# A log-softmax on one core: the first three tiles are stored at once, the later ones half a tile late

## The chip, the core and the metric

The kernel runs on one core of a Trainium2 chip. The metric is device time in microseconds (us) of one launch. Ten runs of the kernel before the change gave 7587.55 to 7592.54 us, with a median of 7589.58 us.

## What is computed

The reference takes `x` of shape 16 x 512 x 50000 in float32 and computes a log-softmax over the last axis:

```
max_x = np.max(x, axis=-1, keepdims=True)
shifted = x - max_x
log_sum_exp = np.log(np.sum(np.exp(shifted), axis=-1, keepdims=True))
return shifted - log_sum_exp
```

Input and output have 1638.4 MB each. Every byte is read once and written once, so some 3277 MB pass between HBM and SBUF.

## The kernel before

**Tiling.** The 8192 rows of 50000 numbers are cut into 256 tiles of 32 rows. A row lies on four neighbouring partitions (G = 4), so a tile is 128 partitions x 12500 numbers, 6250 KB (6.4 MB). There are four buffers of that size in SBUF (NBUF = 4); tile t lives in buffer t mod 4, is loaded into it, changed in place and stored from it. Inside a tile the work on the numbers goes in four column pieces of 3125 (NS = 4).

**One tile, engine by engine.**

- SyncE (SP) issues the load (L147). The first four loads need no wait. Each later load into a buffer waits until the store from that buffer has landed (`take(sync, stored[j])`, L47).
- VectorE (DVE) waits for the landing (L47) and takes the negated maximum of each of the four pieces (L197). Some small instructions then agree on one maximum per row (L202, L165, L168, L174, L180).
- ScalarE (ACT) computes the exponentials of a piece, with their sum, as soon as the maximum of that piece is there (L239, four per tile). It then computes four correction factors (L247).
- DVE multiplies sums by factors (L208), TensorE adds them up across a row's partitions (L277), ACT takes the logarithm (L227), and DVE subtracts maximum and logarithm from the whole tile in place (L185).
- The store is a DMA that ACT issues (L231). It waits on the semaphore `subtracted` until DVE has subtracted that tile.

**Order.** Each engine has its own program and runs it in order; the semaphores tie them together. There is no scheduler: the order on each engine is the one written. On DVE the tiles follow one another without interleaving: maxima of tile t, subtraction of tile t, maxima of tile t+1. On ACT the store of a tile stands inside the work of the next tile, between its second and its third exponential (GATE = 2):

```
for c in range(NS):
    if c == GATE and dst is not None:
        store((j - 1) % NBUF, dst, bufs[(j - 1) % NBUF])
    shifted.next(scalar.activation(out=dump, ...))
```

So the store of tile t is issued only after half of the exponentials of tile t+1. The last tile is different: it is subtracted and stored in four pieces, and the store of the tile before it is put ahead of its exponentials.

**Loops.** DVE and TensorE run a loop of 63 rounds of four tiles and then four more tiles written out. SP writes out the first four loads and loops 63 times over four loads. ACT writes out tile 0, loops 63 times over four tiles (1, 2, 3 and 0 of the next four), and writes out the last three. Because semaphores only count up, each engine ends a round with `settle`, which waits for what it has counted and takes that amount off again.

Loads go through the queue that the profile calls q1, stores through q10.

Of the kernel before, what the change touches and what calls it, by code (L numbers as in the profile page):

```python
# [19 lines left out]
NBUF = 4  # L20
# [29 lines left out]
def cols(c):  # L50
    return slice(c * C, (c + 1) * C)
# [3 lines left out]
def kernel(  # L55
# [11 lines left out]
    ntiles = N // R  # L67


    rounds = (ntiles - NBUF) // NBUF  # L70
# [3 lines left out]
    ot = of.rearrange("(t r) (g w) -> t (r g) w", r=R, g=G)  # L74

    def run(a, first, n):

        part = a[first : first + NBUF * n].rearrange("(q i) p w -> q i p w", i=NBUF)
        return lambda q, i: part[bass.ds(q, 1), i].rearrange("o p w -> (o p) w")
# [13 lines left out]
    bufs = [data.tile([P, W], FP32, name=f"buf{j}") for j in range(NBUF)]  # L93
# [37 lines left out]
    @block.gpsimd  # L131
    def _(gpsimd):
        view = ones.rearrange("p (r g) -> p r g", g=G)
        gpsimd.memset(ones, 1.0).then_inc(ready)  # L134
        gpsimd.affine_select(  # L135
            out=view, in_=view, pattern=[[-G, R], [0, G]], base=0,
            channel_multiplier=1, compare_op=ALU.is_ge, fill=0.0,
        ).wait_op(ready, 1, "sem-ge").then_inc(ready)
        gpsimd.affine_select(  # L139
            out=view, in_=view, pattern=[[G, R], [0, G]], base=G - 1,  # L140
            channel_multiplier=-1, compare_op=ALU.is_ge, fill=0.0,
        ).wait_op(ready, 2, "sem-ge").then_inc(ready)
# [80 lines left out]
    @block.scalar  # L223
    def _(scalar):
        def log(k):
            added.next(
                scalar.activation(out=logs[k], in_=rowsums[k], func=ACT.Ln)  # L227
            ).then_inc(logged.sem)

        def store(j, dst, buf):  # L230
            subtracted.next(scalar.dma_start(out=dst, in_=buf)).then_inc(stored[j], 16)  # L231

        def whole(j, dst=None):
# [4 lines that stand above are left out]
                shifted.next(  # L238
                    scalar.activation(  # L239
                        out=dump, in_=bufs[j][:, cols(c)], func=ACT.Exp,  # L240
                        bias=negms[j][:, c : c + 1], scale=1.0,
                        accum_out=parts[j][:, c : c + 1],
                    )
                ).then_inc(on_act.sem)
                on_act.next(scalar.nop())  # L245
            agreed.next(
                scalar.activation(  # L247
                    out=scales[j], in_=negms[j], func=ACT.Exp,
                    bias=negmaxs[j][:, 0:1], scale=-1.0,
                )  # L250
            ).then_inc(rescaled.sem)
            log(j)

        def settle():
            for count in (on_act, shifted, agreed, added, subtracted):
                count.settle(scalar)

        nc.scalar.preload_act_table_set("natural_log_exp_and_others")  # L258
        whole(0)
        settle()  # L260
        dst = run(ot, 0, rounds)
        with scalar.Fori(0, rounds) as q:
            for i in range(NBUF):
                whole((i + 1) % NBUF, dst(q, i))
            settle()
        for t in range(ntiles - NBUF + 1, ntiles - 1):
            whole(t % NBUF, ot[t - 1])
        store(t % NBUF, ot[t], bufs[t % NBUF])
        whole(NBUF - 1)
        for c in range(NS):  # L270
            store(NBUF - 1, ot[ntiles - 1][:, cols(c)], bufs[NBUF - 1][:, cols(c)])
# [50 lines left out]
```

## Time and profile before

| what | value |
|---|---|
| median of 10 runs | 7589.58 us (7587.55 to 7592.54) |
| the profiled execution | 7589.23 us, span 7587.5 us |
| DVE busy | 5440.4 us, 72% of the span |
| ACT busy | 3184.6 us, 42% |
| PE busy | 477.8 us, 6% |
| maxima, L197 | 1024 times, 3400 ns each |
| exponentials, L239 | 1024 times, 2868 ns each |
| subtraction of a whole tile, L185 | 6.79 us |
| bytes | 1638.40 MB read, 1638.40 MB written, 432 GB/s over the span |
| loads, issue to landing | median 36.7 us |
| stores of whole tiles, issue to landing | median 41.6 us |

The span is the time that the profile covers; 1.7 us of the profiled execution lie outside it. Busy time of an engine counts the instructions that compute; issuing a DMA and waiting are not in it. In the rows of windows further down, the columns are: the stretch in us from the span's start, its length, the busy time of PE, PE's weight loads, DVE, ACT and POOL with the number of instructions, TensorE's granted clock, the mean busy share of the 16 DMA engines, and GB/s. In the rows of a timeline they are: start, duration, engine, line, operation, output and inputs; in square brackets stands the idle time ahead of it and what ended it.

### The profile page before, as it was taken

How to read it: one execution, taken by the hardware profiler on the slowest of the kernel's cores; microseconds unless marked ns; L12 is line 12 of the kernel's file. 1: busy time of each engine (PE TensorE's matmuls, PEld its weight loads, DVE VectorE, ACT ScalarE, POOL GpSimd, SP SyncE). 2: the span in 40 equal slices, each digit the busy share in tenths (PEclk: the TensorE clock that was granted, in tenths of full speed). 3: DMA queues.
4: the chain of work that ended last, by engine and by line, in shares of the span. 5: the costliest groups of instructions: out<-in, count | busy, mean ns of one | idle time of the engine just before them, and what ended most of it. 6: DMA issues, size and time to landing. Idle time of an engine off the chain costs nothing. (4 is left out here: it accounts for less than half of the span.)

```text
span 7587.5 us, 13821 instructions
## 1 busy us (share of the span) xinstructions
PE 477.8 (6%) x2048; PEld 455.9 (6%) x2048; DVE 5440.4 (72%) x2819; ACT 3184.6 (42%) x2561; POOL 1.4 (0%) x7
## 2 busy tenths in 40 slices
PE   0000000000000000000000000000000000000000
PEld 0000000000000000000000000000000000000000
DVE  7777777777777777777777777777777777777776
ACT  4434444344443434444344443434444344444433
POOL 0000000000000000000000000000000000000000
DMA  9999999999999999999999999999999999999999
GB/s 417 433 433 431 433 434 432 433 434 433 433 434 434 431 434 434 432 433 434 434 432 434 434 432 434 434 432 434 434 434 432 434 433 432 434 434 431 434 434 399
DMA packets 74162, 3276.85 MB, mean 432 GB/s; under 512 B 8240, under 2 KB 8240, under 8 KB 8240
## 3 DMA queue, kind: packets, MB, share of 16 engines
q1 hardware_dynamic: 36864, 1638.42, 50.0%
q10 hardware_dynamic: 37296, 1638.42, 50.0%
q14 instruction: 2, 0.02, 0.0%
HBM read 1638.40 MB, written 1638.40 MB: 432 GB/s over the span
## 5 line engine op out<-in xcount | busy, mean ns | idle before, releaser
L239 ACT ACTIVATE dump<-buf,negm 128x3125 f32<-128x3125 f32 x1024 | 2937.3, 2868 | 3804.4 <-DVE negm L197 3765.0
L197 DVE TENSOR_REDUCE negm<-buf 128x1 f32<-128x3125 f32 x1024 | 3418.2, 3400 | 922.7 <-DVEq L47 922.7
L185 DVE TENSOR_SCALAR buf<-buf,negmax,logsum 128x12500 f32<-128x12500 f32 (+1 forms) x259 | 1738.8, 6714 | 553.6 <-ACT logsum L227 553.6
L277 PE MATMUL sums<-scaled,ones 128*128 128x1 f32 x2048 | 477.8, 355 | 7086.5 <-DVE scaled L208 7086.5
L277 PEld LDWEIGHTS sums<-scaled,ones 128*128 128x128 f32 x2048 | 455.9, 327 | 7108.3 <-DVE scaled L208 7108.3
L208 DVE TENSOR_TENSOR scaled<-scale,part 128x4 f32<-128x4 f32 x256 | 41.6, 162 | 580.4 <-ACT scale L247 580.4
L227 ACT ACTIVATE logsum<-sums 128x1 f32<-128x1 f32 x256 | 43.8, 171 | 550.9 <-PE sums L277 550.9
L239 ACT ACTIVATION_READ_ACCUMULATOR dump<-buf,negm 128x1 f32 x1024 | 190.8, 186 | 0.0
L247 ACT ACTIVATE scale<-negm,negmax 128x4 f32<-128x4 f32 x256 | 76.1, 297 | 23.6
L202 DVE TENSOR_REDUCE negp<-negm 128x1 f32<-128x4 f32 x256 | 40.1, 157 | 39.2 <-DVE negm L197 39.2
L180 DVE STREAM_TRANSPOSE negmax<-spread 128x32 f32<-128x32 f32 x256 | 54.2, 212 | 8.9
L165 DVE STREAM_TRANSPOSE allneg<-negp 128x32 f32<-128x32 f32 x256 | 54.1, 211 | 8.9
L168 DVE TENSOR_REDUCE rowneg<-allneg 128x8 f32<-128x32 f32 x256 | 47.6, 186 | 8.9
L174 DVE COPY spread<-rowneg 128x32 f32<-128x32 f32 x256 | 46.3, 181 | 8.9
L258 ACT ACT_TABLE_LOAD x1 | 1.3, 1283 | 1.0 <-SPq L111 1.0
L139 POOL TENSOR_SCALAR_AFFINE_SELECT ones<-ones 128x128 f32<-128x128 f32 x1 | 0.5, 520 | 0.1
L135 POOL TENSOR_SCALAR_AFFINE_SELECT ones<-ones 128x128 f32<-128x128 f32 x1 | 0.5, 519 | 0.1
L134 POOL MEMSET ones<- 128x128 f32 x1 | 0.2, 205 | 0.5 <-SPq L111 0.5
L306 POOL MEMSET const-uint8-127<- 128x1 uint8 x1 | 0.1, 103 | 0.0
L306 POOL MEMSET const-bfloat16-1.0<- 128x1 bf16 x1 | 0.1, 102 | 0.0
L306 POOL MEMSET const-float32-0.0<- 128x1 f32 x1 | 0.1, 100 | 0.3 <-issue 0.3
L306 POOL MEMSET const-float32-1.0<- 128x1 f32 x1 | 0.1, 100 | 0.0
## 6 DMA issues: line engine op xcount, KB each, us to landing
buf<-in_x_dram SPq DMA_DIRECT2D x256, 6250.0 KB, 36.7
out_dram<-buf ACTq DMA_DIRECT2D x255, 6250.0 KB, 41.6
out_dram<-buf ACTq DMA_DIRECT2D x4, 1562.5 KB, 11.3
```

What stands on the lines that cost most here:

```text
L165: vector.transpose(out=allneg, in_=negp.to_broadcast([P, SQ]))
L168: vector.tensor_reduce(out=rowneg, in_=allneg.rearrange("p (r g) -> p r g", g=G), op=ALU.min, axis=AX,)
L174: vector.tensor_copy(out=spread.rearrange("p (r g) -> p r g", g=G), in_=rowneg[:, :, None].to_broadcast([P, SQ // G, G]),)
L180: vector.transpose(out=negmaxs[k], in_=spread)
L185: ins = vector.tensor_scalar(out=buf, in0=buf, scalar1=negmaxs[k][:, 0:1], scalar2=logs[k], op0=ALU.add, op1=ALU.subtract,)
L197: vector.tensor_reduce(out=negms[j][:, c : c + 1], in_=bufs[j][:, cols(c)], op=ALU.max, axis=AX, negate=True,).then_inc(shifted.sem if c < ...
L202: vector.tensor_reduce(out=negp, in_=negms[j], op=ALU.min, axis=AX).then_inc(on_dve.sem)
L208: vector.tensor_mul(out=scaleds[j], in0=scales[j], in1=parts[j])
L227: scalar.activation(out=logs[k], in_=rowsums[k], func=ACT.Ln)
L239: scalar.activation(out=dump, in_=bufs[j][:, cols(c)], func=ACT.Exp, bias=negms[j][:, c : c + 1], scale=1.0, accum_out=parts[j][:, c : c + 1],
L247: scalar.activation(out=scales[j], in_=negms[j], func=ACT.Exp, bias=negmaxs[j][:, 0:1], scale=-1.0,)
L277: ins = tensor.matmul(rowsums[j], ones, scaleds[j][:, c : c + 1], start=c == 0, stop=c == NS - 1,)
```

## The change

Only ACT's program changes. Tiles 0, 1 and 2 are stored as soon as DVE has subtracted them: on ACT, the store of tile t now stands right behind the logarithm of tile t and ahead of the first exponential of tile t+1. From tile 3 on a store stands where it stood, between the second and the third exponential of the next tile.

For this, four tiles instead of one are written out ahead of ACT's loop, the loop has 62 rounds instead of 63 and goes over tiles 0, 1, 2 and 3 of a round, and four tiles instead of three are written out behind it. `settle` on ACT now follows the last tile of a group of four, where it followed the first one. There are 259 store DMAs as before, to the same places; the programs of SP, DVE, TensorE and GpSimd are the same.

```
         nc.scalar.preload_act_table_set("natural_log_exp_and_others")
-        whole(0)
+
+        for t in range(NBUF - 1):
+            whole(t)
+            store(t, ot[t], bufs[t])
+        whole(NBUF - 1)
         settle()
-        dst = run(ot, 0, rounds)
-        with scalar.Fori(0, rounds) as q:
-            for i in range(NBUF):
-                whole((i + 1) % NBUF, dst(q, i))
+        dst = run(ot, NBUF - 1, rounds - 1)
+        with scalar.Fori(0, rounds - 1) as q:
+            for j in range(NBUF):
+                whole(j, dst(q, j))
             settle()
-        for t in range(ntiles - NBUF + 1, ntiles - 1):
+        for t in range(ntiles - NBUF, ntiles - 1):
             whole(t % NBUF, ot[t - 1])
         store(t % NBUF, ot[t], bufs[t % NBUF])
         whole(NBUF - 1)
```

## The prediction

> **What bounds the kernel now.** I read the page from the top: slices, then queues, then the waits, then short windows at both ends of the span.
>
> ```profile
> DMA  9999999999999999999999999999999999999999
> GB/s 417 433 433 431 433 434 432 433 434 433 433 434 434 431 434 434 432 433 434 434 432 434 434 432 434 434 432 434 434 434 432 434 433 432 434 434 431 434 434 399
> q1 hardware_dynamic: 36864, 1638.42, 50.0%
> q10 hardware_dynamic: 37296, 1638.42, 50.0%
> ```
>
> The 16 DMA engines are busy in every slice, half for loads (q1) and half for stores (q10), at 431 to 434 GB/s. Only the first and the last slice are lower: a slice is 7587.5/40 = 189.7 us, so the first lacks 189.7 x (1 - 417/433) = 7 us and the last 189.7 x (1 - 399/433) = 15 us. No compute engine bounds it: in the view of waits DVE's maxima wait for landings (L47) in 251 of 256 tiles, 922.7 us in all. In the steady part, load issues follow each other by 29.55 us (load 128 at 3754.78, load 250 at 7360.46: 3605.7/122), while DVE alone needs 25.9 (a first maximum at 44.93, the next tile's at 70.82). So time can be won only where the DMA engines stand idle. The first place, in windows:
>
> ```profile
> 74.00:76.00 2.00, 0.00 (x0) 0.00 (x0) 2.00 (x2) 1.75 (x1) 0.00 (x0) 1.00 1.15 500
> 76.00:78.00 2.00, 0.00 (x0) 0.00 (x0) 2.00 (x2) 1.68 (x3) 0.00 (x0) 1.00 0.52 225
> 78.00:80.00 2.00, 0.00 (x0) 0.00 (x0) 2.00 (x1) 2.00 (x1) 0.00 (x0) 1.00 0.49 150
> 80.00:82.00 2.00, 0.00 (x0) 0.00 (x0) 2.00 (x2) 1.44 (x3) 0.00 (x0) 1.00 0.76 250
> 82.00:84.00 2.00, 0.00 (x0) 0.00 (x0) 2.00 (x1) 2.00 (x2) 0.00 (x0) 1.00 1.00 400
> ```
>
> From 76 to 82 us both queues run dry (last column). In finer windows the two from 77 to 79 move nothing. The reason is in the timeline:
>
> ```profile
> 38.22 6.79 DVE L185 TENSOR_SCALAR buf<-buf,negmax,logsum 128x12500 f32<-128x12500 f32 x1 [2.16 <-ACT logsum L227]
> ...
> 48.36 2.87 ACT L239 ACTIVATE dump<-buf,negm 128x3125 f32<-128x3125 f32 x1 [10.18 <-DVE negm L197]
> ...
> 54.84 0.40 ACTq L231 DMA_DIRECT2D out_dram<-buf  x1
> ...
> 80.72 0.35 ACTq L231 DMA_DIRECT2D out_dram<-buf  x1
> ```
>
> Tile 0 is subtracted at 38.22 + 6.79 = 45.01, but its store goes out at 54.84. By 77 loads 0 to 3 and store 0, all that was issued, are through. Store 0 lands at 54.84 + 23.8 = 78.7, load 4 follows at 78.95, and store 1 only at 80.72. The second place is the tail:
>
> ```profile
> 7556.00:7558.00 2.00, 0.00 (x0) 0.00 (x0) 2.00 (x1) 2.00 (x1) 0.00 (x0) 1.00 0.87 375
> 7558.00:7560.00 2.00, 0.00 (x0) 0.00 (x0) 1.64 (x6) 1.62 (x3) 0.00 (x0) 1.00 0.12 50
> ...
> 7564.00:7566.00 2.00, 0.28 (x2) 0.19 (x1) 1.48 (x1) 0.17 (x1) 0.00 (x0) 1.00 0.06 25
> 7566.00:7568.00 2.00, 0.00 (x0) 0.00 (x0) 2.00 (x2) 0.00 (x0) 0.00 (x0) 1.00 0.50 212
> ```
>
> The last load lands at 7545.3 (DVE's last maxima start at 7545.34). From 7558 to 7566 two of 16 DMA engines (0.12) and then one (0.06) still store earlier tiles; the rest wait for tile 255, whose first store piece goes out at 7566.46. From the last landing to the end it is a fixed chain, 7587.5 - 7545.3 = 42.2 us.
>
> **The change part by part.**
>
> *Three stores move forward.* The timeline has subtractions 0, 1 and 2 ending at 45.01, 64.11 + 6.79 = 70.90 and 89.99 + 6.79 = 96.78; the stores go out at 54.84, 80.72 and 106.61, so each moves by 9.8 us. Before 77 that gains nothing: the engines already move 400 to 425 GB/s, and store 0 only takes turns with load 3. The five transfers still end near 77.9, in another order: load 3, now landing at 69.6 (2.43 + 67.1), lands near 77; tile 3's maxima start at 96.70, which leaves 19 us. What changes is that store 1 is in the queue from 71.0 and carries the engines past 77.9 until load 4 joins them. **The hole goes.** Its size: the two empty windows alone are 2.0 us; the shortfall of 76 to 82 against 433 GB/s is (208 + 283 + 183) x 2 / 433 = 3.1 us; with 82 to 90 (400, 400, 375, 350) it adds (33 + 33 + 58 + 83) x 2 / 433 = 1.0, so 4.1. I take 3.0, next to the middle one, and keep 2.0 and 4.1 as ends.
>
> *Is a new hole opened?* One tile takes 14.8 us of the engines (load 1 lands 14.8 after load 0). From 77.9, load 4 and store 1 last to 77.9 + 29.6 = 107.5; store 2 is there from 96.8, load 5 from store 1's landing near 105. Load 5 and store 2 last to 137. Store 3 keeps its place, at 132.49: tile 4's maxima start at 122.58 as before, since load 4, issued at 78 instead of 78.95, lands near 110 (now 78.95 + 31.9 = 110.9). With 1.7 us from issue to the first bytes (store 0 is issued at 54.84, q10's first packets start about 56.5) it is ready at 134.2, 3 us in time. No hole, but this is the tightest place.
>
> *The wait on ACT.* The store, with its wait for DVE, now heads tile t+1's work. Behind it stand four exponentials, the first of which waits for a maximum until 48.36 anyway; the store takes 0.40 us from 45.0 and leaves 2.9 us of cover. Without that cover it would cost 0.4 us a tile, three times, on an engine that is 42% busy. Taken out from between exponentials 2 and 3 it gains nothing: the fourth starts 13.45 us after the first maximum with the store (58.38 - 44.93) and without it (32.48 - 19.03).
>
> *Loop, `settle`, longer program.* `settle` and the loop's branch fall in ACT's 10 us of waiting while DVE subtracts, before and after. ACT's program grows by 17 instructions; the page has 0.02 MB of instruction transfers, which is 0.05 us of DMA. Zero. On SP loads 4 to 6 go out earlier, each behind its own store; nothing else is queued there.
>
> *The end.* The hole's 3.0 us reach the end only if the last landing moves by 3.0, that is if as many stores are still outstanding at that moment as now: 7558 - 7545.3 = 12.7 us of DMA. If none were, the last load would land 12.7 us later; if the idle stretch 7558 to 7566 were filled, 8 us earlier. I take zero: from tile 4 on the two streams keep their distance (store 4 lands at 197.9, load 6 at 175.9: 22.0; store 248 at 7419.3, load 250 at 7397.2: 22.1), and store 3's rule is the old one. Stepping the two queues by turns I get some 23.6 instead of 22 after the change, under 1 us at the end, towards a gain.
>
> Sum: 7589.23 - 3.0 = 7586.2 for the profiled execution; the median lies 0.35 above it, so **7586.6**.
>
> The Trainium skill, "DMA: Bandwidth & Descriptors", section "Issuing engines are not separate DMA queues", says that transfers started by different engines run on the same 16 DMA engines and interleave. The trace agrees: windows of 4 us have 400, 400, 400, 413 and 475 GB/s from 56 to 76, with load 3 and store 0 together, and 413, 425 and 400 from 44 to 56, with loads alone. It speaks against a larger gain: were the queues separate, three stores 9.8 us earlier could give up to 29 us, some 7560.
>
> **The rivals.**
>
> - *No gain at the end: 7589.6.* The hole is filled and comes back near 134 to 137, where I have 3 us to spare, or is lost in the tail. For it: that small margin. Against it: the engines were full from 90 to 190 in every window.
> - *Stores get ahead and the last load lands later: about 7594.* The same bytes pass before it and more of them are stores. At the price of 9.8 us, one store's advance, less 3.0, it would be 7596; half of it 7591.5. It decides once the streams' distance falls well below 22. Against it: the old rule holds from tile 3 on.
> - *The slow step stays, slower by over 0.2%: about 7700.* Load 12 goes out at 317.86 and load 20 at 558.21: 30.04 us a tile, against 29.55 later, so each tile from 8 to 24 lost about 0.5 us, at full queues. Why it ends is not visible. If the new start puts the streams where the step never comes down, some 228 tiles x 0.49 = 112 us are added to 7586.6. It decides if stores land after the next loads are through, distance near 29.5 instead of 22; I get 23.6.
> - *Faster by over 0.2%*, below 7574.4: hole 4.1 and tail 8 together are 12.1 us, so 7577.5 at best. Only something unseen does it.
>
> **How the numbers follow.** Forecast 0.70 (7584 to 7589), no gain 0.12, stores ahead 0.10, slow step 0.06, faster 0.02. A measurement of this kernel tells about 0.2% (15 us) from no change: faster 0.02, slower 0.06, the same 0.92. The range: below, the hole's 4.1 and a little of the tail, 7582; above, no gain and half of the stores-ahead case, 7593. The far ends of the tail (7578.6 and 7599) are outside it, with the slow step; 2 in 10 at most.
>
> **What would show it.** In the changed profile the stores go out near 45.1, 71.0, 96.9 and 132.5; windows 76 to 82 show 400 or more; load 4 goes out near 78; store 248 lands 22 to 24 us after load 250; the last maxima start near 7542.3. I am wrong if a window with under 300 GB/s stands between 100 and 200, if the distance differs by more than 5 us, or if load issues stay at 30 us apart after 1000 us.

## The result, and the profile after

The changed kernel takes **7677.74 us** (median of 9 runs, 7607.86 to 7723.38), against 7589.17 us (30 runs, 7587.55 to 7592.54) for the kernel before. The ratio of the fast runs, which leaves out the one of 7723.38 us, is 1.0097, with a 95% interval of 1.0080 to 1.0114; the two medians alone give 1.0117. Either way it is slower, by the medians by 89 us, where 3 us less were forecast. The runs of the kernel before agree within 5 us; those of the changed kernel are spread over 115. The profiled execution took 7689.64 us, its span is 7687.9.

The page of the changed kernel, slices, queues and DMA issues:

```profile
GB/s 415 432 433 431 432 429 431 426 429 428 425 425 425 428 428 426 425 428 429 428 422 426 428 428 425 425 425 425 429 428 425 425 425 428 425 428 425 429 425 401
q10 hardware_dynamic: 37296, 1638.42, 50.5%
q1 hardware_dynamic: 36864, 1638.42, 49.5%
...
buf<-in_x_dram SPq DMA_DIRECT2D x256, 6250.0 KB, 44.7
out_dram<-buf ACTq DMA_DIRECT2D x255, 6250.0 KB, 35.0
```

Slices two to five move the same 431 to 433 GB/s as before; from the eighth to the last but one the rate is 422 to 429. So the loss is not at the start, where the change was made: it is spread over four fifths of the run. The stores' queue q10 now takes more time than q1 for the same bytes (50.5% against 49.5%). And the times in flight have changed places: loads 44.7 us instead of 36.7, stores 35.0 instead of 41.6. The same in windows (the last column is GB/s):

```profile
200.00:600.00 400.00, 24.26 (x104) 23.15 (x104) 285.97 (x146) 162.05 (x131) 0.00 (x0) 1.00 1.00 433
600.00:1000.00 400.00, 24.27 (x104) 23.15 (x104) 286.73 (x151) 173.37 (x139) 0.00 (x0) 1.00 1.00 432
1000.00:2500.00 1500.00, 93.34 (x400) 89.06 (x400) 1062.54 (x550) 620.83 (x499) 0.00 (x0) 1.00 1.00 427
2500.00:5000.00 2500.00, 156.81 (x672) 149.61 (x672) 1767.96 (x915) 1033.39 (x834) 0.00 (x0) 1.00 1.00 426
```

The DMA engines count as busy all the time (1.00) and still move less. They are not idle; some packets take longer. The trace has each packet, that is each piece that a DMA engine moves at a time. A packet of a whole tile is one partition's 50000 bytes and takes 1.847 us in most cases; what the packets took beyond that, summed and shared out over 16 engines, is:

```
us beyond 1.847 a packet, per DMA engine    loads   stores   total
before                                       10.0      5.6    15.7
changed                                      19.2    100.0   119.2
```

119.2 - 15.7 = 103.5 us, which is the 100.4 us by which the span grew (7687.9 - 7587.5) and some 3 us for the hole at the start that went. **The cost is in the store packets.** Which ones, the time of their start tells. Store packets of the changed kernel between 2000 and 7400 us, by the time from the latest issue of a store to the packet's start:

```
start after issue, us   1.0-1.2  1.2-1.4  1.4-1.6  1.6-1.8  1.8-2.0  2.0-2.2  2.2-2.4  2.4-2.6  2.6-2.8
packets                      39       38       37      179      365      574      577      465      290
over 0.15 us too long        3%      45%      78%      99%     100%     100%      77%       4%       0%
mean beyond 1.847, ns         7      347      654      874      840      781      522       22        2
```

A store packet that an engine begins 1.4 to 2.4 us after the store is issued takes some 0.8 us longer (0.52 to 0.87 by the last row). One that begins later doesn't. In the kernel before, no store packet of those 5400 us begins between 1.2 and 2.2 us after an issue, and four between 2.2 and 2.4: 1.3 us after an issue 14 of the 16 engines are in a load packet, and nearly all turn to the store at 2.4 us or later.

At the start, the change did what it says, in the changed kernel's timeline and windows:

```profile
45.10 0.39 ACTq L231 DMA_DIRECT2D out_dram<-buf  x1
...
70.98 0.34 ACTq L231 DMA_DIRECT2D out_dram<-buf  x1
```

```profile
60.00:64.00 4.00, 1.86 (x8) 1.78 (x8) 0.16 (x1) 1.76 (x4) 0.00 (x0) 1.00 0.84 262
76.00:78.00 2.00, 0.00 (x0) 0.00 (x0) 2.00 (x2) 1.68 (x3) 0.00 (x0) 1.00 1.09 375
78.00:80.00 2.00, 0.00 (x0) 0.00 (x0) 2.00 (x1) 2.00 (x1) 0.00 (x0) 1.00 0.85 350
80.00:82.00 2.00, 0.00 (x0) 0.00 (x0) 2.00 (x2) 1.68 (x3) 0.00 (x0) 1.00 0.99 425
```

The stores go out at 45.10 and 70.98, and the hole from 76 to 82 us is filled (350 to 425 GB/s, where 150 to 250 stood). But 60 to 64 has 262 GB/s, where it had 400 before. From 57 to 77 us all 16 engines take turns between load 3 and store 0 in step, and most store packets there are 0.3 to 0.7 us too long. Load 3 lands at 83.7 and load 4 goes out at 84.14, later than before (78.95), not sooner. What the hole had cost is lost ahead of it.

In what follows, the **distance** is how long store t lands after load t+2. Before it stays at 22.1 us. In the changed kernel it is 19.1 for tiles 3 to 5, 15.8 at tile 20 and 15 from tile 30 on.

### The profile page after: what moved, and what is told of

Read it like the earlier page. It is cut to its first block, busy times and chain, and to the rows that moved or that the text cites. A ratio compares the mean times of both kernels' runs of the same rounds, so it can differ in the third digit from the quotient of the medians.

```text
span 7687.9 us, 13810 instructions
## 1 busy us (share of the span) xinstructions
PE 477.9 (6%) x2048; PEld 455.9 (6%) x2048; DVE 5440.4 (71%) x2819; ACT 3184.7 (41%) x2561; POOL 1.4 (0%) x7
## 3 DMA queue, kind: packets, MB, share of 16 engines
q10 hardware_dynamic: 37296, 1638.42, 50.5%
q1 hardware_dynamic: 36864, 1638.42, 49.5%
## 6 DMA issues: line engine op xcount, KB each, us to landing
buf<-in_x_dram SPq DMA_DIRECT2D x256, 6250.0 KB, 44.7
```

## The experiments

Several theories were set against each other in turn; each is named, with a letter, in the expectation of the run that tests it. One execution of each kernel was profiled; the table, worked out from the traces, is for tiles 150 to 244. A store is "in flight" from its issue to its landing. "Early" are store packets that begin 1.2 to 2.4 us after a store's issue, counted per tile over 16 engines; "too long" is over 0.15 us.

```
                        us a    distance  store in   early     of these   us beyond 1.847
                        tile       us     flight us  packets   too long   a tile and engine
before                  29.55     22.1      41.6       0.0         -          0.04
changed                 30.03     15.0      35.0      10.2        90%         0.53
loop only               29.57     22.2      41.7       1.0        10%         0.06
first only              30.02     18.6      38.7       8.9        88%         0.50
third only              29.57     22.2      41.7       0.8        15%         0.06
before, one pad         29.55     22.1      41.3       0.2        33%         0.05
changed, two pads       29.58     22.1      41.1       1.2        46%         0.07
changed, all late       30.36     22.8      34.0       9.4        92%         0.82
before, late load       29.59     25.2      44.7       0.8         0%         0.04
changed, late stores    29.87     19.1      39.2       5.3        80%         0.27
changed, gate 1         29.67     14.8      37.6       2.3        72%         0.17
before, gate 3          30.01     22.5      39.2       9.0        80%         0.51
all at once             29.58     14.8      47.7       3.1         0%         0.02
changed, gate 0         29.57     14.8      47.7       5.1         0%         0.01
```

The first column and the last one go together in every row: a tile takes about as much more than 29.5 us as its packets are too long.

### Which part of the change

**Loop only**: the new loop with the old stores.

```
-        for t in range(NBUF - 1):
-            whole(t)
-            store(t, ot[t], bufs[t])
-        whole(NBUF - 1)
+        whole(0)
+        whole(1, ot[0])
+        whole(2, ot[1])
+        whole(3, ot[2])
```

> The loop, the place of settle and the written-out tiles are those of the changed kernel, but tiles 0, 1 and 2 are stored after half of the next tile, as before the change. Theory A (the early stores set a packet phase between loads and stores that then persists; the loop itself costs nothing): as fast as before, 7587 to 7592 us, with stores landing 22 us after the load two tiles on. Rival C (the rotated loop or the longer program of ACT costs the time): as slow as the changed kernel, 7610 to 7720 us.

Measured: 7590.74 us (10 runs, 7588.77 to 7591.82), ratio 1.0001 (0.9991 to 1.0010), distance 22.2. Neither the loop nor the longer program costs anything.

**First only**: tile 0 is stored at once, tiles 1 and 2 as before.

```
         whole(0)
+        store(0, ot[0], bufs[0])
-        whole(1, ot[0])
+        whole(1)
         whole(2, ot[1])
         whole(3, ot[2])
```

> Only tile 0 is stored at once; tiles 1 and 2 wait for half of the next tile. Theory A: whichever start puts the two streams at another distance than 22 us may be slow; store 0 alone changes where load 3 lands, so I expect a distance near 19 us and 7610 to 7720 us; should it come out at 22 us, then 7590. Rival B (only the filled hole at 77 us matters, that is store 1 going out early): store 1 stays at 80.7 us, the hole stays, 7587 to 7592 us.

Measured: 7699.20 us (4 runs, 7668.96 to 7703.74), ratio 1.0145 (1.0129 to 1.0162). The distance is 18.7 at tile 8 and 18.4 at tile 20. Store 0 alone does all of it, though store 1 stays at 80.95. Its page:

```profile
GB/s 412 432 433 434 434 434 432 433 433 432 433 434 433 431 426 425 426 426 426 425 425 426 426 426 426 430 428 424 425 426 426 427 428 423 429 426 426 427 428 398
```

The rate falls in the fifteenth slice, near 2700 us, and not at the start: a start that moves the two streams makes the slow pattern possible, and the run falls into it later.

**Third only**: tile 2 alone is stored at once.

```
-        whole(3, ot[2])
+        store(2, ot[2], bufs[2])
+        whole(3)
```

> Only tile 2 is stored at once; tiles 0 and 1 wait for half of the next tile, so store 0 starts at 54.8 us and the hole at 77 us stays. Theory D: the distance depends on store 0 beginning in step with load 3; here it does not, so 22 us and 7587 to 7592 us. Rival B2 (each early store costs): 7600 us or more.

Measured: 7589.40 us (4 runs, 7587.12 to 7590.90), ratio 0.9999 (0.9985 to 1.0014), distance 22.2. An early store as such costs nothing. Store 0 does, which meets load 3; store 1 alone was not tried.

### Is it the moment of the store's issue, or the distance

Two kernels put a tiny activation on ACT, once or twice, ahead of each store that stands between exponentials.

```
                 if c == GATE and dst is not None:
+                    for _ in range(2):
+                        scalar.activation(
+                            out=pad, in_=negms[j][:, 0:1], func=ACT.Exp, scale=0.0
+                        ).then_inc(on_act.sem)
+                        on_act.next(scalar.nop())
                     store((j - 1) % NBUF, dst, bufs[(j - 1) % NBUF])
```

**Changed, two pads:**

> The changed kernel with two tiny activations on ACT ahead of each store from tile 3 on, which put these stores off by about 0.9 us against the landing that releases them. In the changed kernel's trace nearly all store packets that start 1.2 to 2.4 us after a store's issue take 0.5 to 0.9 us longer, and hardly any other packet does. Theory A1 (this start phase is the cost): 0.9 us later the packets ahead fall otherwise, first store packets start after 2.4 us, the slow ones go, 7587 to 7600 us. Rival A2 (the distance of 15 us between the streams is itself the cost): the distance stays, 7610 to 7720 us.

**Before, one pad:**

> The kernel before with one tiny activation on ACT ahead of each store, which puts stores off by about 0.45 us. In the trace of before the first store packets start 2.6 to 3.0 us after the issue and none is slow. Theory A1: they now start at 2.1 to 2.6 us, many in the slow stretch, so 7600 to 7720 us. Rival A2 (distance): stays at 22 us, so 7588 to 7593 us.

Measured: 7643.71 us with two pads on the changed kernel (7 runs, 7604.13 to 7707.95; ratio 1.0075, 1.0040 to 1.0110) and 7589.45 us with one pad on the kernel before (10 runs, 7588.45 to 7591.88). Neither came out as theory A1 had it; both medians lie where rival A2 had them. The pads were worth less than I had put them at: a store follows the landing of the next tile by 10.29 us with one and by 10.52 with two, instead of 10.05. So A1 was not put to a fair test. But the profiled execution with two pads (span 7614.0) shows something better, the change from one pattern to the other within one run:

```profile
200.00:600.00 400.00, 24.28 (x104) 23.16 (x104) 286.34 (x146) 167.01 (x157) 0.00 (x0) 1.00 1.00 433
600.00:1000.00 400.00, 24.34 (x105) 23.23 (x105) 287.27 (x152) 179.54 (x167) 0.00 (x0) 1.00 1.00 432
1000.00:2500.00 1500.00, 95.15 (x408) 90.77 (x408) 1063.52 (x551) 642.26 (x601) 0.00 (x0) 1.00 1.00 428
2500.00:5000.00 2500.00, 156.83 (x672) 149.65 (x672) 1793.48 (x926) 1078.68 (x1008) 0.00 (x0) 1.00 1.00 432
5000.00:7400.00 2400.00, 151.24 (x648) 144.29 (x648) 1725.44 (x893) 1042.44 (x973) 0.00 (x0) 1.00 1.00 433
```

The rate is 428 between 1000 and 2500 us, 432 from there to 5000 and back at 433 after that. The distance goes with it: 19.3 at tile 4, 15.6 at tile 30, 19.3 at tile 80, 22.1 from tile 100 on. So the next theory, D, was the distance: 22 us is fast, 15 to 19 slow.

**Changed, late stores**: the stores of tiles 99 to 102 alone go behind the next tile's logarithm (shown are the four tiles that stand between the two halves of the loop).

```
+        for j in range(NBUF):
+            whole(j, ot[NBUF - 1 + NBUF * AT + j], late=True)
+        settle()
```

> The changed kernel, but the stores of tiles 99 to 102 alone are issued behind the logarithm of the next tile, which pushes the distance between the streams above 19.3 us; all other stores are as in the changed kernel. Theory D: the first 100 tiles are as in the changed kernel, from tile 103 on the distance is 20 us or more and a tile takes 29.55 us; 7590 to 7640 us. Rival B2: no difference to the changed kernel, 7610 to 7720 us, and 30.0 us a tile to the end.

Measured: 7634.70 us (4 runs, 7594.53 to 7656.29), ratio 1.0053 (1.0025 to 1.0082), which both ranges hold, so the trace decides. The shift worked: the distance was 15.4 at tile 80 and 25.7 at tile 100, and the tiles from 104 to 178 took 29.6 to 29.7 us each. But it did not hold: the distance was 17.7 at tile 200 and 14.8 at tile 248, and the last 50 tiles took 30.0 to 30.1. By this trace D would be right on what is fast, and wrong that a distance lasts.

**Before, late load**: load 100 is made late (shown are the lines ahead of it; the loop is split there).

```
+            if j == 0:
+                for _ in range(2):
+                    sync.dma_start(out=tiny, in_=xt[0][:, 0:1]).then_inc(tiny_in, 16)
+                    take(sync, tiny_in)
             load(j, xt[NBUF * (AT + 1) + j])
```

> The kernel before with one disturbance: ahead of load 100, SP moves two tiny transfers (512 bytes each) and waits for each, which makes this one load late by some 8 to 12 us. Its early tiles are stored as before. Theory D: from there the distance is below 20 us and each of the last 150 tiles takes 30.0 instead of 29.55 us in most executions, 7640 to 7680 us. Rival B2 (only the early stores cost) and rival E (what is lost is lost in the first 1000 us): the late load costs at most its own delay, 7588 to 7602 us.

Measured: 7604.36 us (4 runs, 7600.71 to 7605.77), ratio 1.0019 (1.0005 to 1.0033). The disturbance was larger than meant: load 100 went out 33.7 us later than in the trace of before and landed 14.3 us later. I had the direction wrong, too: the distance went up, to 25.4, and stores were then 44.7 us in flight at 29.59 us a tile. The late load cost its own delay and no more. It leaves D standing, since 25 is not a small distance, but is no proof of it.

**Changed, all late**: every store from tile 3 on goes behind the next tile's logarithm (shown is its new place; the old one is switched off).

```
             log(j)
+            if dst is not None:
+                store((j - 1) % NBUF, dst, bufs[(j - 1) % NBUF])
```

> The changed kernel with its three early stores, but every later store is issued behind the logarithm of the next tile instead of between its exponentials. A store then follows the landing that releases it by about 19.3 us, so stores cannot land less than 19.3 us after the load two tiles on, and the patterns at 14.8 and 18.5 us are shut out. Theory D (the distance between the two streams, kept from the start, decides: 22 us gives 29.55 us a tile, 15 to 19 us gives 30.0): 7583 to 7595 us. Rival B2 (the early stores cost time in themselves, whatever comes later): 7610 us or more.

Measured: 7784.31 us (4 runs, 7722.71 to 7800.44), ratio 1.0242 (1.0204 to 1.0279). **D falls here**: the distance is 22 to 24 us, as in the fast kernels, and this is the slowest of all. Stores are 34.0 us in flight, and 92% of 9.4 early packets a tile are too long. Its time is in B2's range, but the third-only kernel speaks against B2, by which the early stores cost in themselves, and so does the next pair, where the kernel before gets as slow without any early store. What I took to be left is the store's own time: it is issued too late against the work that the DMA engines still hold. That is theory F.

### When the store is issued against the work in the queues

**Changed, gate 1** and **before, gate 3** each change one number.

```
-GATE = 2
+GATE = 1
```

> The changed kernel, with each store from tile 3 on between the first and the second exponential of the next tile instead of the second and the third, that is some 3.3 us sooner after the landing that releases it (6.6 instead of 9.9 us). Theory F (what decides is how early the store is issued against the work that the DMA engines still hold: stores of 41 us or more in flight are fast, below 39 slow, because a store packet that begins 1.2 to 2.4 us after the store's issue takes 0.8 us longer): the start gives a distance near 19 us, so a store is in flight 29.55 + 19 - 6.6 = 42 us, fast, 7585 to 7593 us. Theory D (the distance of 19 us is slow by itself): 7610 to 7720 us.

> The kernel before, with each store between the third and the fourth exponential, some 3.3 us later after the landing that releases it (13.2 instead of 9.9 us). Theory F: the distance stays near 22 us, so a store is in flight 29.55 + 22 - 13.2 = 38.4 us, slow, 7610 to 7790 us, with store packets that begin 1.2 to 2.4 us after an issue in every tile. Theory D: at 22 us it is fast, 7587 to 7595 us.

The kernel before with GATE = 3 takes 7676.45 us (4 runs, 7652.26 to 7777.93), ratio 1.0100 (1.0078 to 1.0122): as slow as the changed kernel, with the old start, at a distance of 22.5. Its page:

```profile
GB/s 413 433 433 434 434 434 434 434 434 433 430 427 427 427 423 428 426 426 429 426 426 426 429 426 426 426 426 426 429 426 426 426 426 429 426 429 425 426 426 402
q10 hardware_dynamic: 37296, 1638.42, 50.4%
q1 hardware_dynamic: 36864, 1638.42, 49.6%
```

It runs at 433 to 434 GB/s up to the tenth slice and then drops, with q10 taking the longer part, as in the changed kernel.

The changed kernel with GATE = 1 takes 7591.69 us (10 runs, 7574.12 to 7605.21), ratio 1.0001 (0.9991 to 1.0010), at a distance of 15 to 20 us: fast, where D had 7610 or more. F's figure was not met to the end: stores were 42.3 us in flight at tile 8 but 37.9 from tile 20 on, and 2.3 early packets a tile cost 0.1 us a tile late in the run. The trace is that of the slowest of the ten runs.

**All at once**: every tile is stored as soon as it is subtracted (shown is the loop). **Changed, gate 0** sets GATE to 0 in the changed kernel and comes to the same order by that kernel's loop.

```
+        with scalar.Fori(0, rounds) as q:
+            for j in range(NBUF):
+                whole(j)
+                store(j, dst(q, j), bufs[j])
+            settle()
```

> Every tile is stored as soon as it is subtracted, not the first three alone; the last tile goes in four pieces as before. A store is then issued some 3.6 us before the next landing. Theory F: it is in flight 29.55 + 19 + 3.6 = 52 us, its first packets wait behind earlier ones, fast, 7583 to 7593 us. Theory D: the start is that of the changed kernel, the distance 19 us or less, so 7610 us or more.

> The changed kernel, with each store from tile 3 on ahead of the first exponential's successor slot: it stands ahead of the first exponential of the next tile, so it is issued as soon as that tile before it is subtracted, since ACT waits only for the subtraction there. In effect every tile is stored at once, in the changed kernel's own loop. Theory F: as the kernel that stores every tile at once, within 5 us of it, and fast. Rival C2 (the form of the loop matters): another time than that kernel's.

Measured: 7583.63 us for the first (10 runs, 7576.91 to 7584.08), ratio 0.9988 (0.9979 to 0.9998); 7583.69 us for the second (10 runs, 7575.44 to 7606.62), ratio 0.9986 (0.9962 to 1.0009). Both beat the changed kernel. The first also beats the one before, by 0.1%; for the second the interval does not exclude that it is the same. This is the changed kernel's start with none of its cost. The Trainium skill, "DMA: Bandwidth & Descriptors", section "Rules for kernel authors", advises to issue a DMA early, so that its fixed setup overlaps with other work. The times agree with the advice, 7583.63 us with stores at once against 7676.45 with stores behind three of the next tile's four exponentials; the reason that these runs show is another one, the time of store packets (0.02 against 0.51 us a tile and engine), and no run here shows what the setup adds. The page of all at once:

```profile
GB/s 415 434 434 434 433 434 434 434 433 434 434 434 434 432 434 434 434 433 434 434 434 434 432 434 434 434 433 433 434 434 434 432 434 433 434 434 433 434 432 395
...
buf<-in_x_dram SPq DMA_DIRECT2D x256, 6250.0 KB, 44.1
out_dram<-buf ACTq DMA_DIRECT2D x255, 6250.0 KB, 47.7
```

A store is 47.7 us in flight, 18 more than a tile's 29.6: it is issued while much of the store ahead of it is still to come. There are 3.1 early packets a tile here too, and not one is too long. The reading that fits all 14 traces is: the first packet of a store takes some 0.8 us longer on an engine that has no earlier store packets left and turns to the new store 1.4 to 2.4 us after its issue. With earlier stores still queued (all at once), or load packets that hold the engine past 2.4 us (before), it costs nothing.

The landings bear this out, since the trace has them for each of the 16 engines. In tiles 5 to 249 of the 14 traces, 894 stores are issued while the store ahead is still to land on all 16 engines 2.4 us later: 3982 early packets, which must be the store ahead's, and none is too long. At 2106 stores it is still to land on three engines at most 1.2 us after the issue: 8936 early packets, 7406 of them too long, and of those that begin after 1.4 to 2.2 us 5261 of 5447. First only goes from the one case to the other within its run:

```
first only, tiles                     5-24  25-44  45-64  65-84  85-104  105-124
us a tile                            29.64  29.52  29.60  29.86   30.02    30.05
distance, us                          18.4   18.4   18.4   18.5    18.7     18.6
store in flight, us                   37.9   37.9   37.9   38.5    38.6     38.7
engines that hold the store ahead     16.0   16.0   16.0   11.2     1.0      1.0
early packets a tile                   5.0    5.8    6.3    3.0     8.2     11.0
of these too long                      0.0    0.0    0.0    0.2     6.8      9.0
last engine behind the first, us       6.8    6.7    6.7    7.7    17.7     17.6
```

(Engines that hold the store ahead: 2.4 us after the issue. The last row is taken at a load's landing.) Distance and time in flight are nearly the same in its fast and its slow tiles, so neither of them decides; both go by the last engine alone. What changes is on how many engines the store ahead is still queued. It falls when one engine gets further behind the rest: the next load and store wait for that one, while the others finish what they hold. That this is why the queue runs empty is argued from the rows; no run changed it by itself.

## Why the prediction was wrong

- **What bounds the kernel, and 29.55 us a tile:** right. Every fast kernel has it, and all of the loss is DMA time.
- **The three stores move by 9.8 us, ACT's wait, loop and `settle` are free:** right (45.10, 70.98; loop only 7590.74).
- **"The hole goes", 3.0 us:** the hole went, the gain did not come. I let store 0 and load 3 take turns at full rate and end at 77.9. Load 3 landed at 80.8 on the first engine and at 83.7 on the last. Most store packets that all engines begin in step took 0.3 to 0.7 us longer (262 GB/s from 60 to 64 us), and 26 packets of store 1 began before the last engine was through. Up to 110 us the packets lost 6.5 us per engine beyond their 1.847, against 4.0 before.
- **"The end": the streams keep their distance, 23.6 by my stepping.** This is the step that failed. The distance came out at 19, since load 3 landed over 6 us later than I had it, and went on to 15. Stores were then in flight for 35 us and not 42. I took the DMA engines' rate to be the same whenever a store is issued and let the distance matter only in the tail, so my sum has nothing for the tiles in between. There the loss is: once the store ahead is through on most engines when the next one is issued, store packets take longer, 0.48 us a tile (30.03 against 29.55), and some 200 tiles make 96 of the 100.4 us. The distance as such is not the cause: all late is slow at 22.8 us and all at once fast at 14.8.
- **The rivals.** "The slow step stays" named the course and nearly the size (30.04 us a tile, 7700 us), at a chance of 0.06. The size is luck. In the trace of before, the 30 us a tile from tile 8 to 24 are no lower DMA rate: 237 to 475 us has 434 GB/s and 475 to 712 has 432, and packets are less than 0.1 us a tile too long. Load issues are further apart there as the last engine falls behind, from 2.9 us behind the first at load 8 to 12.2 at load 24, which is 0.58 us a tile. And I put the rival at a distance near 29.5, where loads would run dry; it came from the other side, where stores run dry.
- **"No hole is opened" and the tail:** right, the first with a wrong reading in it. The 1.7 us from issue to the first bytes are not in the trace of before: store 0 is issued at 54.84 and its first packet starts at 59.04, 4.2 us later, so the margin was 0.3 us and not 3. Between 110 and 200 us no DMA engine stands idle for more than 0.4 us in the changed kernel's trace. From the last landing to the end it is 39 us (7687.9 - 7648.9), where it was 42.2.

Still open is why one engine falls behind, why the engines, once in the slow pattern, mostly stay there (one run with two pads left it, the one with late stores fell back), and why store packets begun in step cost 0.3 to 0.7 us at 57 to 77 us. That the empty store queue makes the first packet long rests on the counts above; no run changed it alone, and what in the engine takes the time is not shown. One run out of 25 of the kernel before, beside the last four kernels, took 7671.39 us: it may have fallen into the slow pattern as well, but there is no trace of it.

## What to carry to other kernels

When transfers bound a kernel and both directions run at once, "all DMA engines busy" is no ceiling: compare the time of one packet and what is still queued at each issue between kernels, not only the busy share. Keep the next transfer queued behind the one ahead of it (here: store at once, 47.7 us in flight at 29.6 us a tile) instead of timing it to arrive when the engines come free. And a change at the start of a long loop whose buffers feed each other can set a pattern that lasts for the whole run, so its price is a rate times all tiles, not the microseconds at the start.

## What the runs showed of the hardware

- A store packet of 50000 bytes takes 1.847 us, but mostly 2.5 to 2.9 us, 2.68 in the median, when it starts 1.4 to 2.2 us after its store's issue on an engine without earlier store packets (5261 of 5447; with the store ahead still on all engines, 0 of 2585).
- One or two of 16 DMA engines fall behind the others and stay behind: in the kernel before, load 128 lands on 14 engines by 3779 us, on the next at 3787.4 and on the last at 3791.7; the landing that everything waits for is that one, 16 us behind the first from load 40 on. In the tail one engine alone is busy (a share of 0.06 is one of 16), in the changed kernel too:

```profile
7658.00:7660.00 2.00, 0.00 (x0) 0.00 (x0) 2.00 (x2) 1.68 (x3) 0.00 (x0) 1.00 0.93 400
7660.00:7662.00 2.00, 0.00 (x0) 0.00 (x0) 2.00 (x1) 1.99 (x2) 0.00 (x0) 1.00 0.06 25
7668.00:7670.00 2.00, 0.00 (x0) 0.00 (x0) 1.90 (x2) 0.07 (x1) 0.00 (x0) 1.00 0.06 25
```

- Distances between the streams often settle at steps of two packets: 22.1, 18.4 and 14.8 us, where 2 x 1.847 is 3.7. That of late load, 24.5 to 25.4, is not on such a step.
